# A hybrid decoder block on one core: GpSimd's elementwise work of the SSM stage moved to VectorE

## Chip, cores and metric

One core of one Trainium2 chip (trn2) runs the whole program in one launch. The metric is device time in microseconds (us), lower is better. Engines carry the names of the profile: PE (TensorE), PEld (its weight loads), DVE (VectorE), ACT (ScalarE), POOL (GpSimd) and SP (SyncE, which only issues DMAs here).

## What is computed

One decoder layer, 1024 tokens of 1024 features, all in float32. Cut to the parts that matter here:

```python
h = _rmsnorm(x, norm_mix_g[l])
z = h @ w_in[l]
q, k, v, f, u_ssm, g_attn, g_ssm = jnp.split(z, splits, axis=-1)
y_attn = _forgetting_attention(q, k, v, f + b_forget[l])
y_ssm = _s5(u_ssm, ...)
mixed = sigmoid(g_attn) * (y_attn @ w_proj_attn[l]) + sigmoid(g_ssm) * (y_ssm @ w_proj_ssm[l])
x = x + mixed @ w_out[l]
x = x + _hier_moe(...)
```

`_s5` is a diagonal state-space model of 32 groups, each with 16 channels and 64 complex states: x_t = A x_(t-1) + B u_t, y_t = Re(C x_t) + D u_t, then GELU and a gated linear unit. The two gates g_attn and g_ssm are 2 x 1024 columns of the first product.

## The kernel before

The program goes through stages: norm and the product for u and the forget gate; **the SSM stage**, in which the gate products also run; attention with its projections; the output projection and the router; the 32 experts. The change lies in the SSM stage, about 65 to 320 us of the trace.

Matrix products that must be exact use split operands. Each weight tile is cast on ACT to a high part (`wgh`, L149), and the remainder (`wgl`, raw minus high, L150) is a low part; a product is then three matmuls per block of 128 rows: high by high (L160), low by high (L161), high by low (L162), each 512 columns wide. `gate_run(m)` does this for 128 of the 2048 gate columns: 2 x 24 matmuls. The weights come in groups of 256 columns, as two raw tiles `raw_g` of 128 x 1024 values; `gate_split` casts and subtracts both, one subtraction on DVE and one on POOL. A group is split a group ahead, and its raw slots are then free for the next load, which SP issues (L103). The finished gate tile is copied out of PSUM on ACT (`ge`, L164) and stored by a DMA from ACT's queue (L165).

The state-space part runs in four blocks of 8 groups (here called the first to the fourth). Tiles of a block have one buffer each, so blocks follow each other. In a block:

- DVE makes phases `v` and `CO` (L518 to L525), with two wraps to a whole turn (L283, L284); ACT takes their sines (`SI` L524, `CO` L526). `w` shares its memory with `zc`, so the first wrap of a block waits until PE has read the `zc` of the block before.
- `outer` (L533 to L539) makes `HQ` (128 x 1152) and `PT` (128 x 1024): a product on DVE, a second product into `tq` on POOL (L538), and the sum on DVE.
- PE multiplies `HQ` (L551) into `Ka`, copied out by ACT (L554), corrected by DVE (L556) and spread into `Mt` by eight DMAs from POOL's queue (L558). PE transposes `PT` (L577), ACT copies it out as `Pm` (L581), and PE multiplies `Pm` with the inputs (L584).
- `turn` (L561 to L567) rotates this by the phases into `zin`, for each half of the block: products on DVE (L564, L566, the latter into `zt`) and the sum on POOL (L567). DVE scans `zin` along time (L596), `turn` rotates back into `zc`, and PE multiplies `Mt` and `zc` into the outputs (L604, L605), through GELU on ACT (L608).

A tile scheduler sets the order on every engine when the program is built, from its own estimate of times. On PE it puts the gate matmuls between those of the blocks. Each engine then runs its list strictly in that order: a matmul whose operand is late holds the gate matmuls behind it too.

Of the kernel before, what the change touches and what calls it, by code (L numbers as in the profile page):

```python
# [16 lines left out]
ALU = mybir.AluOpType  # L17
# [25 lines left out]
def hybrid_block(ctx: ExitStack, tc: tile.TileContext, t, out):  # L43

    nc = tc.nc
# [20 lines left out]
    def f32(ap):  # L66
        return ap.bitcast(F32)
# [4 lines left out]
    def slot(name, shape=(S,), dt=F32, where=None):  # L72
        pl, n = where or (slab, SLOTS)
        return pl.tile([P] + list(shape), dt, tag="s4", name=name, bufs=n)
# [69 lines left out]
    def gate_split(raws):  # L144
        ws = []
        for kh, raw in enumerate(raws):
            wh = slot("wgh", (4, 256), F32R)
            wl = slot("wgl", (4, 256), F32R)
            nc.scalar.copy(wh, raw)  # L149
            (nc.gpsimd if kh else nc.vector).tensor_tensor(wl, raw, f32(wh), ALU.subtract)  # L150
            ws.append((wh, wl))
        return ws

# [282 lines left out]
    def gate_run(m):  # L436

        g = m // 2
        if m % 2 == 0:
            if g + 1 not in gates and g + 1 < 8:  # L440
                gates[g + 1] = gate_split(raw_gs[g + 1])
            if g + 2 < 8:
                raw_gs.append(gate_load(g + 2))
        for n in range(2):
            gate_products(m, gates[g], n)
# [4 lines left out]
    for g in range(2):  # L450
        gates[g] = gate_split(raw_gs[g])
# [36 lines left out]
    with ExitStack() as st:  # L488
# [19 lines left out]
        for b in range(G // GB):  # L508
# [22 lines left out]
            tq = wp2.tile([P, GB, 9, CG], F32, name="tq", tag="t3")  # L531

            def outer(dst, ua, ca, ub, cb, op, n, n0):  # L533
                sh = [P, GB, n, CG]
                ub4 = lambda u_: u_[:, gs, n0:n0 + n].unsqueeze(3).to_broadcast(sh)
                cb4 = lambda c_: c_[:, gs, :].unsqueeze(2).to_broadcast(sh)
                nc.vector.tensor_tensor(dst, ub4(ua), cb4(ca), ALU.mult)
                nc.gpsimd.tensor_tensor(tq[:, :, 0:n, :], ub4(ub), cb4(cb), ALU.mult)  # L538
                nc.vector.tensor_tensor(dst, dst, tq[:, :, 0:n, :], op)  # L539

            outer(HQ, U1g, Cre, U2g, Cim, ALU.add, 9, 0)
            outer(PT, U1r, Bbr, U2r, Bbi, ALU.add, 8, 0)

            Mt = wp2.tile([P, GB, P], F32, name="Mt")
# [16 lines left out]
            def turn(dst, src, sl, op):  # L561
                zt = wp2.tile([P, 4, P], F32, name="zt", bufs=2)
                n = src.shape[2]
                nc.vector.tensor_tensor(dst, src, CO[:, sl, 0:n], ALU.mult)  # L564
                for o in (0, 64):
                    nc.vector.tensor_tensor(zt[o:o + 64, :, 0:n], src[64 - o:128 - o], SI[o:o + 64, sl, 0:n], ALU.mult)  # L566
                nc.gpsimd.tensor_tensor(dst, dst, zt[:, :, 0:n], op)  # L567


            zin = wp2.tile([P, GB, P], F32, name="zin")  # L570
# [1 line left out]
            for q4 in range(GB // 4):  # L572
                sl = slice(q4 * 4, q4 * 4 + 4)
                psp = smtile()
                for r in range(4):
                    g = q4 * 4 + r
                    nc.tensor.transpose(psp[:, r * P:(r + 1) * P],  # L577
                                        PT[:, g].rearrange("p t c -> p (t c)"), ident)
                v4 = lambda ap: ap.rearrange("p (a b) -> p a b", a=4)
                Pm = wp2.tile([P, 4, P], F32, name="Pm")  # L580
                nc.scalar.copy(Pm, v4(psp))  # L581
                px = smtile()
                for r in range(4):
                    nc.tensor.matmul(px[:, r * P:(r + 1) * P], Pm[:, r, :], uT[:, q4 * 4 + r, :],  # L584
                                     start=True, stop=True)
                turn(zin[:, sl, :], v4(px), sl, ALU.subtract)
# [6 lines left out]
            for q4 in range(GB // 4):  # L593
                sl = slice(q4 * 4, q4 * 4 + 4)
                rs = smtile()
                nc.vector.tensor_tensor_scan(rs, rho[:, sl].rearrange("p g j -> p (g j)"),  # L596
                                             zin[:, sl].rearrange("p g j -> p (g j)"),
                                             0.0, op0=ALU.mult, op1=ALU.add)
                turn(zc[:, sl, 1:P], v4(rs)[:, :, 0:P - 1], sl, ALU.add)
                ps = smtile()  # L600
                for r in range(4):
                    g = q4 * 4 + r
                    o = ps[:, r * P:(r + 1) * P]
                    nc.tensor.matmul(o, uT[:, g, :], Mt[:, g, :], start=True, stop=False)  # L604
                    nc.tensor.matmul(o, zc[:, g, :], HQ[:, g, 1:9, :].rearrange("p n c -> p (n c)"),  # L605
                                     start=False, stop=True)
                c0 = (g0 + q4 * 4) * CG
                nc.scalar.activation(  # L608
                    Yg[:, :, c0:c0 + 64].rearrange("p t (g c) -> p g t c", c=CG),
                    ps.rearrange("p (g t c) -> p g t c", g=4, t=8), AF.Gelu_apprx_tanh)  # L610
# [6 lines left out]
    with ExitStack() as st:  # L617
# [3 lines left out]
        for k in (0, 2):  # L621
            raw = slot("raw_l", (2, 512))
# [18 lines left out]
        for m in range(4):  # L641
            ms = slice(m * P, m * P + P)
            for n in range(2):
                ns = slice(n * 512, n * 512 + 512)
                ps = smtile()
                for k in range(4):
                    wh, wl = [w_[:, k % 2, ms] for w_ in wgl_[k // 2]]
# [870 lines left out]
```

## Time and profile before

| | |
|---|---|
| Three runs | 1191.03, 1191.19, 1195.45 us; median 1191.19 us |
| Profiled execution | 1195.19 us, its span 1193.5 us |
| Busy over the span | PE 1111.4 us (93%), DVE 795.3 (67%), ACT 620.3 (52%), POOL 431.3 (36%) |
| Granted PE clock, mean | 0.974 of full speed |

The profiled execution stands at the slow end of the three runs, 4.0 us above their median; the other 1.7 us beside the span are start and end of the launch. In the timeline a row is one instruction (or several alike, xN): start, duration, engine, line, operation, output and inputs, shapes; in brackets the time its engine stood idle before it and what ended that. A 512-column matmul shows 0.39 us but a new one starts every 0.23 us, as they are pipelined. The granted clock is a share of full speed: 1.00 is the 2.4 GHz level, 0.50 the 1.2 GHz level.

### The profile page before, as it was taken

The numbers are of one execution on the slowest core, as the hardware profiler recorded it, in microseconds if no ns is written. First come the engines' busy times: TensorE is split into PE (matmuls) and PEld (weight loads), VectorE is DVE, ScalarE is ACT, GpSimd is POOL, SyncE is SP. The second block draws the span as 40 slices with busy tenths as digits, with TensorE's granted clock in tenths as the row PEclk, the third lists the DMA queues.
The fourth block names the chain that finished last, engine by engine and source line by source line (L and its number), as shares of the span: only waits on it lengthen the run. The fifth ranks groups of instructions, "written<-read, shape, count | busy, mean of one in ns | idle before, by whom it ended". The sixth has DMA issues, their size and how long they took to land. (4 is left out here: it accounts for less than half of the span.)

```text
span 1193.5 us, 15934 instructions
## 1 busy us (share of the span) xinstructions
PE 1111.4 (93%) x5323; PEld 851.5 (71%) x5324; DVE 795.3 (67%) x1561; ACT 620.3 (52%) x1195; POOL 431.3 (36%) x431
## 2 busy tenths in 40 slices
PE   5999989899999999999899989998599999999995
PEld 4778877787898878888667767886366666666562
DVE  4976786575027889898986795538566666666661
ACT  5443232233226566756769453103466666666672
POOL 3143553541523564756624362103322222222211
PEclk9999999899999999999999998999699999999998
DMA  7625652330443020001523548564699999999992
GB/s 236 85 55 159 137 81 62 72 90 18 116 96 54 10 43 23 22 13 45 204 71 116 176 152 310 190 221 179 189 329 343 330 309 317 318 309 322 315 331 47
DMA packets 100918, 193.78 MB, mean 162 GB/s; under 512 B 26176, under 2 KB 55168, under 8 KB 100832
## 3 DMA queue, kind: packets, MB, share of 16 engines
q1 hardware_dynamic: 82176, 150.16, 41.1%
q0 software_dynamic: 14048, 34.17, 10.5%
q10 hardware_dynamic: 4608, 8.39, 1.9%
q8 instruction: 43, 0.70, 0.2%
q14 instruction: 43, 0.35, 0.1%
HBM read 164.30 MB, written 35.52 MB: 167 GB/s over the span
## 5 line engine op out<-in xcount | busy, mean ns | idle before, releaser
L1104 DVE TENSOR_TENSOR wel<-raw_e,weh 128x512 fp32r<-128x512 f32 x256 | 157.4, 687 | 118.1 <-ACT weh L1103 118.1
L1103 ACT CAST weh<-raw_e 128x512 fp32r<-128x512 f32 x256 | 137.1, 623 | 1.7 <-DMA raw_e<-in_w_expert_gate 1.3
L912 POOL TENSOR_TENSOR sm<-sm,pe 128x256 f32<-128x256 f32 (+2 forms) x80 | 96.3, 1204 | 69.5 <-ACT pe L909 61.3
L1379 PE MATMUL psA_t<-wd,hT 128*96 128x512 f32 x256 | 117.0, 600 | 2.7 <-DMA wd<-in_w_expert_down 1.9
L1354 PE MATMUL psA_t<-weh,xh 128*96 128x512 f32 x256 | 102.9, 402 | 0.2
L161 PE MATMUL psA_t<-hTh,wgl 128*128 128x512 f32 x256 | 101.8, 398 | 0.0
L160 PE MATMUL psA_t<-hTh,wgh 128*128 128x512 f32 x256 | 101.6, 397 | 0.0
L1355 PE MATMUL psA_t<-wel,xh 128*96 128x512 f32 x256 | 101.5, 396 | 0.0
L162 PE MATMUL psA_t<-hTl,wgh 128*128 128x512 f32 x256 | 101.3, 396 | 0.0
L1356 PE MATMUL psA_t<-weh,xl 128*96 128x512 f32 x256 | 100.6, 393 | 0.0
L1381 POOL DMA_INDIRECT out_rows<-R,ix x32 | 46.0, 1438 | 128.1 <-ACT hT L1370 116.9
L795 PE MATMUL psA_t<-wqh,hTh 128*128 128x384 f32 x256 | 87.9, 343 | 0.0
L796 PE MATMUL psA_t<-wql,hTh 128*128 128x384 f32 x256 | 86.3, 337 | 0.0
L797 PE MATMUL psA_t<-wqh,hTl 128*128 128x384 f32 x256 | 86.2, 337 | 0.0
L1330 POOL DMA_INDIRECT XG<-xn_d,ix x32 | 36.1, 1128 | 136.5 <-PE psB_t L1341 130.6
L1380 ACT ACTIVATE R<-psA_t,wts 96x512 f32<-96x512 f32 x64 | 43.8, 684 | 76.7 <-PE psA_t L1379 74.6
L1379 PEld LDWEIGHTS psA_t<-wd,hT 128*96 128x96 f32 x256 | 40.5, 168 | 55.6 <-issue 49.4
L907 ACT ACTIVATE pH<-psB_t 128x512 fp32r<-128x512 f32 (+1 forms) x96 | 49.2, 512 | 36.4 <-PE psB_t L904 36.2
L910 DVE TENSOR_TENSOR pL<-pe,pH 128x256 fp32r<-128x256 f32 (+2 forms) x80 | 63.0, 800 | 6.6 <-ACT pe L909 5.7
L160 PEld LDWEIGHTS psA_t<-hTh,wgh 128*128 128x128 f32 x256 | 48.5, 190 | 10.0 <-DVE uS L219 0.5
L161 PEld LDWEIGHTS psA_t<-hTh,wgl 128*128 128x128 f32 x256 | 48.7, 190 | 9.7 <-POOL wgl L150 0.2
L1163 PE MATMUL psA_t<-woh,mxh 128*128 128x512 f32 x128 | 54.3, 424 | 1.2 <-DVE gt L988 1.2
(427 smaller groups left out, 2867.8 us busy)
## 6 DMA issues: line engine op xcount, KB each, us to landing
raw_e<-in_w_expert_gate SPq DMA_DIRECT2D x64, 512.0 KB
raw_e<-in_w_expert_up SPq DMA_DIRECT2D x64, 512.0 KB
wd<-in_w_expert_down SPq DMA_DIRECT2D x64, 512.0 KB
gate_d<-ge ACTq DMA_DIRECT2D x32, 256.0 KB
gt<-gate_d SPq DMA_DIRECT2D x16, 512.0 KB
raw_g<-in_w_in SPq DMA_DIRECT2D x12, 512.0 KB
raw_q<-in_w_in SPq DMA_DIRECT2D x48, 128.0 KB
x<-in_x SPq DMA_DIRECT2D x8, 512.0 KB
```

The source lines that it names most:

```text
L160: nc.tensor.matmul(ps, wh, hTh[k][:, ns], start=(k == 0), stop=False)
L161: nc.tensor.matmul(ps, wl, hTh[k][:, ns], start=False, stop=False)
L162: nc.tensor.matmul(ps, wh, hTl[k][:, ns], start=False, stop=(k == KD - 1))
L795: nc.tensor.matmul(ps[:, :384], ah, wh, start=(k == 0), stop=False)
L796: nc.tensor.matmul(ps[:, :384], ah, wl, start=False, stop=False)
L912: nc.gpsimd.tensor_tensor(sm[:, o0:], sm[:, o0:], pe[:, :n], ALU.add)
L1103: nc.scalar.copy(wh[d_], src)
L1104: nc.vector.tensor_tensor(wl[d_], src, f32(wh[d_]), ALU.subtract)
L1354: nc.tensor.matmul(ps, xh[:, k, :], wh[:, k % 2, :], start=(k == 0), stop=False)
L1355: nc.tensor.matmul(ps, xh[:, k, :], wl[:, k % 2, :], start=False, stop=False)
L1356: last = nc.tensor.matmul(ps, xl[:, k, :], wh[:, k % 2, :], start=False, stop=(k == KD - 1))
L1379: pe = nc.tensor.matmul(po, hT[:, j, :], wd[j][:, ns], start=(j == 0), stop=(j == 1))
```

## The change

Three elementwise operations change engine; nothing else in the source does. The second `wgl` of each gate group, the second product of `outer` and the sum of `turn` go from POOL to DVE:

```diff
             nc.scalar.copy(wh, raw)
-            (nc.gpsimd if kh else nc.vector).tensor_tensor(wl, raw, f32(wh), ALU.subtract)
+            nc.vector.tensor_tensor(wl, raw, f32(wh), ALU.subtract)
...
                 nc.vector.tensor_tensor(dst, ub4(ua), cb4(ca), ALU.mult)
-                nc.gpsimd.tensor_tensor(tq[:, :, 0:n, :], ub4(ub), cb4(cb), ALU.mult)
+                nc.vector.tensor_tensor(tq[:, :, 0:n, :], ub4(ub), cb4(cb), ALU.mult)
                 nc.vector.tensor_tensor(dst, dst, tq[:, :, 0:n, :], op)
...
-                nc.gpsimd.tensor_tensor(dst, dst, zt[:, :, 0:n], op)
+                nc.vector.tensor_tensor(dst, dst, zt[:, :, 0:n], op)
```

POOL keeps the memsets of `Mt` and `zc`, the DMAs that fill `Mt`, and `yo` (L654). Because the scheduler orders anew, PE, DVE, ACT and POOL have other lists in this stage; SP's list is the same, and the stages after it are too.

DVE, third block, from the end of `HQ` to the end of `CO`. Before:

```order
L150 TENSOR_TENSOR wgl<-raw_g,wgh 128x1024
L520 TENSOR_TENSOR w<-phl,j_623 128x1024
L539 TENSOR_TENSOR PT<-PT,tq 128x1024
L521 TENSOR_TENSOR v<-w,v 128x1024
L522 TENSOR_SCALAR CO<-v 128x1024
L283 TENSOR_SCALAR w<-v 128x1024
L284 SCALAR_TENSOR_TENSOR v<-w,v 128x1024
L283 TENSOR_SCALAR w<-CO 128x1024
L284 SCALAR_TENSOR_TENSOR CO<-w,CO 128x1024
```

And with the change:

```order
L150 TENSOR_TENSOR wgl<-raw_g,wgh 128x1024
L520 TENSOR_TENSOR w<-phl,j_623 128x1024
L150 TENSOR_TENSOR wgl<-raw_g,wgh 128x1024
L521 TENSOR_TENSOR v<-w,v 128x1024
L538 TENSOR_TENSOR tq<-U2r,Bbi 128x8x128
L522 TENSOR_SCALAR CO<-v 128x1024
L283 TENSOR_SCALAR w<-v 128x1024
L539 TENSOR_TENSOR PT<-PT,tq 128x1024
L284 SCALAR_TENSOR_TENSOR v<-w,v 128x1024
L538 TENSOR_TENSOR tq<-U2g,Cim 128x1152
L283 TENSOR_SCALAR w<-CO 128x1024
L284 SCALAR_TENSOR_TENSOR CO<-w,CO 128x1024
```

Three instructions came in ahead of the last `CO`: the second `wgl`, the `tq` for `PT`, and the `tq` for the `HQ` of the fourth block.

PE, third block, from the products for `Ka` to the first that needs `Pm`. Before:

```order
L551 MATMUL psB_t<-HQ,Bst 16x128 x8
L577 MATMUL psB_t<-ident,PT 128x128 x4
L160 MATMUL psA_t<-hTh_134,wgh 128x512
L161 MATMUL psA_t<-hTh_134,wgl 128x512
L162 MATMUL psA_t<-hTl_142,wgh 128x512
L160 MATMUL psA_t<-hTh_135,wgh 128x512
L584 MATMUL psB_t<-uT,Pm 128x128 x4
```

And with the change:

```order
L551 MATMUL psB_t<-HQ,Bst 16x128 x8
L577 MATMUL psB_t<-ident,PT 128x128 x4
L160 MATMUL psA_t<-hTh_134,wgh 128x512
L161 MATMUL psA_t<-hTh_134,wgl 128x512
L162 MATMUL psA_t<-hTl_142,wgh 128x512
L160 MATMUL psA_t<-hTh_135,wgh 128x512
L161 MATMUL psA_t<-hTh_135,wgl 128x512
L162 MATMUL psA_t<-hTl_143,wgh 128x512
L160 MATMUL psA_t<-hTh_136,wgh 128x512
L161 MATMUL psA_t<-hTh_136,wgl 128x512
L584 MATMUL psB_t<-uT,Pm 128x128 x4
```

The first L584 stands four gate matmuls further back.

ACT, second block, from the sines to the two `Pm`. Before:

```order
L524 ACTIVATE SI<-v,sgn 128x1024
L164 COPY ge<-psA_t 128x512
L526 ACTIVATE CO<-CO 128x1024
L165 DMA gate_d<-ge 128x512
L149 CAST wgh<-raw_g 128x1024
L164 COPY ge<-psA_t 128x512
L149 CAST wgh<-raw_g 128x1024
L165 DMA gate_d<-ge 128x512
L554 COPY Ka<-psB_t 16x512 x2
L581 COPY Pm<-psB_t 128x512 x2
```

And with the change:

```order
L524 ACTIVATE SI<-v,sgn 128x1024
L526 ACTIVATE CO<-CO 128x1024
L164 COPY ge<-psA_t 128x512
L149 CAST wgh<-raw_g 128x1024
L165 DMA gate_d<-ge 128x512
L554 COPY Ka<-psB_t 16x512 x2
L581 COPY Pm<-psB_t 128x512
L149 CAST wgh<-raw_g 128x1024
L581 COPY Pm<-psB_t 128x512
```

One `wgh` cast went from ahead of the first `Pm` to behind it, and one `ge` to ahead of the sines. In the third block ACT's list has `ge` behind `CO` before, and ahead of `CO` with the change.

## Rows read from the trace of the kernel before

**Rows 1.** Windows view, one stretch: length; busy by engine; clock; DMA share; GB/s
```profile
core 0: us, PE busy (x) PEld busy (x) DVE busy (x) ACT busy (x) POOL busy (x), PEclk, DMA share, GB/s
200.00:220.00 20.00, 15.48 (x76) 12.84 (x75) 12.99 (x16) 4.80 (x7) 9.31 (x12) 0.83 0.28 65
```

**Rows 2.** PE's waits, 50 to 340 us: total, times, longest
```profile
PE psB_t L584 <- ACT Pm L581: 6.0, 2, 4.5
PE psB_t L604 <- DMA Mt<-Ka: 2.3, 1, 2.3
PE psB_t L605 <- POOL zc L567: 1.5, 2, 1.0
```

**Rows 3.** Timeline of PE, second and third block
```profile
161.88 1.16 PE L584 MATMUL psB_t<-uT,Pm 128*128 128x128 f32 x8 [1.48 <-ACT Pm L581]
...
165.12 0.48 PE L160 MATMUL psA_t<-hTh,wgh 128*128 128x512 f32 x1
...
179.01 0.77 PE L604 MATMUL psB_t<-Mt,uT 128*128 128x128 f32 x2 [2.30 <-DMA Mt<-Ka]
...
210.95 2.08 PE L584 MATMUL psB_t<-uT,Pm 128*128 128x128 f32 x8 [4.52 <-ACT Pm L581]
...
216.72 0.48 PE L162 MATMUL psA_t<-hTl,wgh 128*128 128x512 f32 x1
```

**Rows 4.** Instructions of single lines: duration in ns min/median/max, first and last start
```profile
L537 DVE TENSOR_TENSOR HQ<-U1g,Cre x4: 1337/1340/1359, 93.8 to 237.8; 128x1152 f32<-128x1152 f32 x4
L567 POOL TENSOR_TENSOR zc<-zc,zt x8: 1277/2256/2311, 128.6 to 270.4; 128x508 f32<-128x508 f32 x8
```

**Rows 5.** Timeline of DVE, 60 to 330 us
```profile
61.16 0.68 DVE L407 TENSOR_TENSOR bt<-Bre,sc 128x512 f32<-128x512 f32 x1
...
110.64 1.23 DVE L284 SCALAR_TENSOR_TENSOR CO<-w,CO 128x1024 f32<-128x1024 f32 x1
...
140.32 1.23 DVE L283 TENSOR_SCALAR w<-v 128x1024 f32<-128x1024 f32 x1 [3.13 <-PE psB_t L605]
...
148.17 1.23 DVE L539 TENSOR_TENSOR PT<-PT,tq 128x1024 f32<-128x1024 f32 x1 [1.82 <-POOL tq L538]
...
150.56 2.53 DVE L522 TENSOR_SCALAR CO<-v 128x1024 f32<-128x1024 f32 x1
...
155.72 1.23 DVE L284 SCALAR_TENSOR_TENSOR CO<-w,CO 128x1024 f32<-128x1024 f32 x1
...
187.02 1.23 DVE L283 TENSOR_SCALAR w<-v 128x1024 f32<-128x1024 f32 x1 [9.03 <-PE psB_t L605]
...
192.97 2.95 DVE L520 TENSOR_TENSOR w<-phl,j 128x1024 f32<-128x1024 f32 x1
195.85 3.41 DVE L539 TENSOR_TENSOR PT<-PT,tq 128x1024 f32<-128x1024 f32 x1
...
200.43 2.53 DVE L522 TENSOR_SCALAR CO<-v 128x1024 f32<-128x1024 f32 x1
...
205.59 1.23 DVE L284 SCALAR_TENSOR_TENSOR CO<-w,CO 128x1024 f32<-128x1024 f32 x1
...
224.26 1.23 DVE L150 TENSOR_TENSOR wgl<-raw_g,wgh 128x1024 fp32r<-128x1024 f32 x1 [5.02 <-ACT wgh L149]
...
246.88 0.69 DVE L522 TENSOR_SCALAR CO<-v 128x1024 f32<-128x1024 f32 x1
```

**Rows 6.** Timeline of ACT, first and third block
```profile
115.90 0.57 ACT L554 COPY Ka<-psB_t 16x512 f32<-16x512 f32 x1 [0.45 <-PE psB_t L551]
...
206.85 1.06 ACT L526 ACTIVATE CO<-CO 128x1024 f32<-128x1024 f32 x1 [0.83 <-DVE CO L284]
...
210.33 0.57 ACT L581 COPY Pm<-psB_t 128x512 f32<-128x512 f32 x1
```

**Rows 7.** First of eight DMAs into Mt, second and third block: KB, us to landing
```profile
Mt<-Ka POOLq DMA_DIRECT2D x1, 64.0 KB, 12.6
...
Mt<-Ka POOLq DMA_DIRECT2D x1, 64.0 KB, 2.2
```

**Rows 8.** The page's part 2, DMA engines: busy tenths in 40 slices
```profile
DMA  7625652330443020001523548564699999999992
```

## The prediction

> **What bounds the kernel now.** I read the profile from the coarse view to the fine one. The busy shares say that PE works 93% of the span; but a share is a mean over stages, so I went to the stage that the change touches. In the windows view the reader should see that even at its worst PE is the fullest engine there: in the 20 us from 200 it is busy 15.48 us, DVE 12.99, POOL 9.31 [rows 1]. In most of the other 20 us stretches from 80 to 280 us PE has no idle time at all. So in this stage time is lost only where PE stands still, or runs at a lower clock; what DVE and POOL take costs nothing until PE waits for it.
>
> The list of PE's waits names three such places in the four blocks [rows 2]: for `Pm` twice, 6.0 us together; once for the DMAs into `Mt`, 2.3 us; twice for `zc`, 1.5 us. PE's timeline shows where they fall: 1.48 us in the second block and 4.52 us in the third for `Pm`, 2.30 us in the second for `Mt` [rows 3]. The long ones cost more than their idle time. After the 4.52 us, PE did the same work from L584 on (sixteen L584 matmuls, four transposes, four gate matmuls) in 216.72 - 210.95 = 5.77 us that took 165.12 - 161.88 = 3.24 us in the second block, and the granted clock, 0.83 of full speed in the mean of the window, was at the lower of its two levels (1.2 GHz) for a part of it [rows 1, 3]. That is 2.5 us more, behind a time in which PE did nothing. After the 1.48 us wait nothing of the kind shows.
>
> Why is `Pm` late? `Pm` is a copy on ACT, and ACT's list has the sine of `CO` ahead of it, which waits for DVE's last `CO`: in the third block DVE ends it at 205.59 + 1.23 = 206.8, ACT starts at 206.85, and `Pm` is reached at 210.33 [rows 5, 6]. So the chain is DVE, then ACT, then PE. DVE needs 19.8 us for it, from the first wrap at 187.02 (the moment PE lets go of `zc`) to 206.8 [rows 5].
>
> **What the change does to this chain.** DVE gets more work. By its own rows a product of 128 x 1152 takes 1.34 us there [rows 4], one of 128 x 1024 1.23 us (the sum of `PT` at 148.17) and one of 128 x 512 0.68 us [rows 5]; one behind another starts some 0.1 us sooner than these durations say. All four blocks together receive 4 x (1.34 + 1.23) for `tq`, 16 x 0.68 for the sums of `turn` and 8 x 1.23 for `wgl`: 31 us over the stage, where DVE stands idle 7 of the 20 us of [rows 1] alone. Capacity is not the question, only what lies in the chain.
>
> *Third block.* Into the stretch of 19.8 us come one `wgl` and two `tq`, about 1.1 + 1.1 + 1.3 = 3.5 us. But three of its instructions took far longer than their kind: 2.95, 3.41 and 2.53 us where others of the same shape took 1.21, 1.23 and 0.69 [rows 5]. They are the three beside which POOL ran `tq` or `wgl`; L522 took 2.53 us in the second and third blocks with a `tq` beside it, and 0.69 us in the fourth, where POOL had none [rows 5]. With POOL's arithmetic gone I take the excess of 5.8 us as gone. The bounds are 0 and 5.8; I choose the upper, as the fourth block is the changed case in all but name. So 19.8 - 5.8 + 3.5 = 17.5, and `CO` is 2.3 us earlier. On ACT, 210.33 - 206.85 = 3.5 us pass from `CO` to `Pm` [rows 6]; the sine takes 1.06 of them and two copies of `Ka` about 1.1, and the remaining 1.4 us belong to `ge` and its store. `ge` is now ahead of `CO`, where its product is done, so I take the 1.4 us off. `Pm` is then 3.7 us earlier. PE wants it four gate matmuls later, 4 x 0.23 = 0.9 us. Together 4.6 us against a wait of 4.52 us: the wait goes, and with it the 2.5 us at the lower clock. As the two sides are that near, I leave 0.4 us as a remainder.
>
> *Second block.* From 140.32 to 155.72 + 1.23 = 16.6 us. Two `tq` add 2.4; the wait for POOL's `tq` (1.8) and the excess of L522 (1.8) go [rows 5]: 15.4 us, 1.2 us earlier. One `wgh` cast stands behind `Pm` now, 1 us more. The wait of 1.48 us goes.
>
> *First and fourth block.* In the first, `CO` comes some 1.3 us later by the same kind of sum, but DVE ended it at 111.9 and ACT's copies of `Ka`, ahead of `Pm`, waited for PE until 115.90 [rows 5, 6]: hidden by PE's gate matmuls, with 115.9 - 111.9 - 1.06 for the sine = 2.9 us to spare. If PE came sooner there, `Pm` would be late in this block too. The fourth has no `tq` for a next block, and `Pm` is not waited for.
>
> *The sums of turn.* POOL took 2256 ns for one [rows 4], DVE 0.68 us. The four sums per block add 2.7 us to DVE, but the chain from L584 to `zc` gets shorter: POOL's sums stood behind its DMA issues and a `wgl`. PE's new list asks for the first `zc` about six matmuls earlier than before, 1.4 us. In the third block I get the second `zc` 0.4 us late, in place of 1.5 us of waits [rows 2]; in the other blocks it comes in time.
>
> *The low parts of the gate weights* are a group ahead of their products, so PE does not wait for them; two of them before the first block lie in time that DVE spends waiting for ACT. Cost nothing, as long as DVE keeps that cover.
>
> *Mt.* Its DMAs stay in POOL's queue. In the second block the first landed after 12.6 us, in the third after 2.2 us [rows 7]; in the second, two loads of `raw_g` ran beside it. Those loads start when `wgl` frees a slot, so they move with the chain, and I keep the wait of 2.3 us as it is. The bounds are gone (a gain of 2.3, and up to 2.5 for the clock, as at the other long wait) and 2.7 us longer. A rule speaks against the change here: the Trainium skill (SBUF — State Buffer, section SBUF: two separate sides) says that the descriptors of a DMA from POOL's queue are written by GpSimd, which VectorE locks out while it runs certain two-port instructions. [...]
>
> **Sum.** 1.5 + 4.5 + 2.5 + 1.5 - 0.4 - 0.4 = 9.2 us. Against the profiled execution: 1195.2 - 9.2 = 1186.0 us. That execution is 4.0 us over the median of the runs; which stall it has that the others lack can't be seen, and it may be `Mt`, which I count as unchanged. Against the median: 1191.2 - 9.2 = **1182.0 us**. After the stage every list is the same, so I expect the rest only to start earlier.
>
> **Rivals.**
> 1. *Mt is late in more blocks.* Both `wgl` of a group now run close together, so two loads of `raw_g` start together, and may meet the `Mt` copies in the first and third block as they did in the second. For it: 12.6 against 2.2 us [rows 7]. Against it: in the first block the same meeting cost no wait. Two more waits of 2.3 us with up to 2.5 us of slow clock are 4.6 to 9.6 us: 1186.6 to 1191.6, centre 1189.
> 2. *A cast holds DVE (slower).* `wgl` waits for ACT's `wgh`. DVE stood 5.02 us for one at 224.26 [rows 5]; the second of the pair waited on POOL, where little was behind it. Now both stand in DVE's list between the parts of `turn`, so that a late cast delays `zc`, and PE. It decides if casts come over 1 us later than DVE reaches them. At 5.0 us idle and 2.5 us of slow clock, in the first and third block, this costs 15 us: 1191.2 - 9.2 + 15 = 1197. Against it: with PE's long wait gone, the slot for the cast is free about 7 us sooner, before DVE arrives.
> 3. *The gain is swallowed later.* The DMA engines are busy 90% or more in nine of the last ten slices [rows 8]; if the expert loads do not start sooner, the end stays: 1191. Against it: they wait for slots that earlier work frees, and that moves along.
>
> **How the numbers follow.** Forecast 0.66, rival 1 0.16, rival 2 0.10, rival 3 0.08. The forecast's own range is 1177 (the `Mt` wait gone too, 4.8 us) to 1186 (half of the third block's `Pm` wait and slow clock left, 3.5 us); to leave out no more than 2 in 10, the range has to reach over rival 1: 1176 to 1190. A measurement of this kernel tells about 0.5%, 6.0 us, from no change. The forecast is faster by more than that (0.66); rivals 1 and 3 lie within (0.24); rival 2 is slower (0.10).
>
> **What would show it.** Right: PE's waits for `Pm` and for `zc` are each under 1 us, no stretch of low clock around the third block's L584, L522 at 0.69 us in all blocks, the span of the third block's chain on DVE near 17.5 us. Wrong: L522 still at 2.5 us (then the long rows were not POOL's doing, and `CO` is 3.5 us later); waits of DVE for `wgh` inside `turn`; new waits of PE for `Mt`; or a stage that ends 9 us earlier and a total that does not.

## The result and the profile after

The changed kernel takes **1180.22 us** in the median (6 runs, 1177.96 to 1186.2), the kernel before 1193.43 us (6 runs, 1191.03 to 1195.45): a ratio of 0.9891, with a 95% interval of 0.9867 to 0.9915, so it is 0.9 to 1.3% faster. The forecast was 1182.0 us, faster. The profiled execution took 1180.84 us, against 1195.19 before.

Where the time came from is read from the start of three groups of PE: the first product for `Ka` (L551, first block), the first projection of attention (L795) and the first product of the experts (L1354). After, by single lines (duration in ns, count, first and last start, form):

```profile
L551 PE MATMUL psB_t<-HQ,Bst x64: 272/273/284, 113.7 to 240.6; 128*16 128x128 f32 x64
L795 PE MATMUL psA_t<-wqh,hTh x256: 331/335/423, 319.3 to 558.7; 128*128 128x384 f32 x128
L1354 PE MATMUL psA_t<-weh,xh x256: 387/397/740, 838.0 to 1156.8; 128*96 128x512 f32 x128
```

And before:

```profile
L551 PE MATMUL psB_t<-HQ,Bst x64: 272/273/283, 114.8 to 255.2; 128*16 128x128 f32 x64
L795 PE MATMUL psA_t<-wqh,hTh x256: 331/334/423, 334.2 to 574.2; 128*128 128x384 f32 x128
L1354 PE MATMUL psA_t<-weh,xh x256: 387/394/742, 852.9 to 1171.0; 128*96 128x512 f32 x128
```

From L551 to L795, the SSM stage (called its length below), it is 319.3 - 113.7 = 205.6 us in place of 219.4: 13.8 us less. The experts start 14.9 us sooner, the span ends 14.3 us sooner. So nearly all of the gain in these two executions arises in the stage that was changed, and all but 0.6 us of it is carried to the end.

PE's waits after, 50 to 340 us (the answer to [rows 2]): those for `Pm` and `zc` are gone, that for `Mt` is half of what it was.

```profile
PE psB_t L604 <- DMA Mt<-Ka: 1.2, 1, 1.2
```

The windows after, with the columns of [rows 1]: in the stretch from 200 us PE is busy all 20 us in place of 15.48, POOL 4.58 in place of 9.31, and the granted clock is 1.00 in place of 0.83.

```profile
160.00:180.00 20.00, 18.82 (x101) 15.73 (x99) 15.27 (x22) 4.04 (x6) 2.88 (x6) 1.00 0.67 91
200.00:220.00 20.00, 20.00 (x108) 17.08 (x107) 16.67 (x23) 6.82 (x10) 4.58 (x8) 1.00 0.44 86
```

The chain on DVE in the third block, after (the answer to [rows 5]):

```profile
181.46 1.24 DVE L283 TENSOR_SCALAR w<-v 128x1024 f32<-128x1024 f32 x1 [5.70 <-PE psB_t L605]
...
187.42 1.21 DVE L520 TENSOR_TENSOR w<-phl,j 128x1024 f32<-128x1024 f32 x1
188.56 1.21 DVE L150 TENSOR_TENSOR wgl<-raw_g,wgh 128x1024 fp32r<-128x1024 f32 x1
...
190.82 1.21 DVE L538 TENSOR_TENSOR tq<-U2r,Bbi 128x1024 f32<-128x1024 f32 x1
191.96 0.68 DVE L522 TENSOR_SCALAR CO<-v 128x1024 f32<-128x1024 f32 x1
...
193.16 1.21 DVE L539 TENSOR_TENSOR PT<-PT,tq 128x1024 f32<-128x1024 f32 x1
...
195.43 1.35 DVE L538 TENSOR_TENSOR tq<-U2g,Cim 128x1152 f32<-128x1152 f32 x1
...
197.42 1.22 DVE L284 SCALAR_TENSOR_TENSOR CO<-w,CO 128x1024 f32<-128x1024 f32 x1
```

The three long rows are now 1.21 (L520), 1.21 (L539) and 0.68 us (L522); before they were 2.95, 3.41 and 2.53. From the first wrap to the end of `CO` it is 198.64 - 181.46 = 17.2 us in place of 19.8, with three instructions more in it. ACT starts `CO`'s sine at 198.68 and, with `ge` now ahead of it, reaches `Pm` 1.9 us later in place of 3.5 [rows 6]:

```profile
198.68 1.06 ACT L526 ACTIVATE CO<-CO 128x1024 f32<-128x1024 f32 x1 [0.55 <-DVE CO L284]
...
200.60 0.57 ACT L581 COPY Pm<-psB_t 128x512 f32<-128x512 f32 x1
```

`Pm` is done at 200.60 + 0.57 = 201.17, and PE takes it without a wait, 0.46 us later, when its list comes to it:

```profile
201.63 1.05 PE L584 MATMUL psB_t<-uT,Pm 128*128 128x128 f32 x8
```

So not all of the third block's gain is DVE's. The chain gave 19.8 - 17.2 = 2.6 us, ACT's list with `ge` ahead of `CO` gave 3.5 - 1.9 = 1.6, and the four gate matmuls that PE's list now has ahead of L584 gave 0.9: about half of it comes from the new order.

### The profile page after: what moved, and what is told of

It is laid out like the page before. It is cut to its first block, busy times and chain, and to the rows that moved or that the text cites. A ratio compares the mean times of both kernels' runs of the same rounds, so it can differ in the third digit from the quotient of the medians.

```text
span 1179.2 us, 15928 instructions
## 1 busy us (share of the span) xinstructions
PE 1106.0 (94%) x5323; PEld 848.4 (72%) x5324; DVE 804.9 (68%) x1593; ACT 620.3 (53%) x1195; POOL 356.9 (30%) x399
## 3 DMA queue, kind: packets, MB, share of 16 engines
q0 software_dynamic: 14048, 34.17, 10.6%
## 5 line engine op out<-in xcount | busy, mean ns | idle before, releaser
L1354 PE MATMUL psA_t<-weh,xh 128*96 128x512 f32 x256 | 103.8, 406 | 0.2
L795 PE MATMUL psA_t<-wqh,hTh 128*128 128x384 f32 x256 | 88.0, 344 | 0.0
L164 ACT COPY ge<-psA_t 128x512 f32<-128x512 f32 x32 | 18.7, 584 | 86.6 <-PE psA_t L162 81.8
L857 DVE TENSOR_REDUCE mx<-psB_t 128x1 f32<-128x512 f32 (+2 forms) x96 | 51.2, 551 | 6.2 <-PE psB_t L855 2.7
```

The costliest lines, as they stand in the source:

```text
L795: nc.tensor.matmul(ps[:, :384], ah, wh, start=(k == 0), stop=False)
L1354: nc.tensor.matmul(ps, xh[:, k, :], wh[:, k % 2, :], start=(k == 0), stop=False)
```

## Experiments

Theory A: POOL's arithmetic stretches the DVE instructions beside it, DVE's chain to `CO` ends late, and through ACT's list `Pm` and PE are late. The main rival, B: the new lists alone do it, as the change moved PE's and ACT's instructions too. Ratios stand against runs of the kernel before on the same chip; "length" is that of the stage as above, from one profiled execution each (two of the changed kernel gave 205.6 and 205.8).

| kernel | median us | ratio, 95% interval | length us |
|---|---|---|---|
| tq alone | 1182.79 | 0.9922, 0.9889 to 0.9955 | 206.9 |
| turn sums alone | 1192.16 | 0.9994, 0.9972 to 1.0016 | 215.3 |
| second wgl alone | 1193.3 | 0.9995, 0.9974 to 1.0016 | 217.5 |
| tq and turn sums | 1180.41 | 0.9891, 0.9866 to 0.9916 | 206.2 |
| changed, 12 idle POOL products a block | 1200.21 | 1.005, 1.0022 to 1.0078 | 225.3 |
| the same, in 24 pieces | 1192.1 | 0.9982, 0.9959 to 1.0006 | 215.4 |
| before, CO's sine behind Pm | 1191.53 | 0.9982, 0.9957 to 1.0007 | 213.7 |
| changed, once more | 1183.75 | 0.9912, 0.9894 to 0.993 | 205.8 |
| changed, Mt copies by SP | 1179.87 | 0.9877, 0.9859 to 0.9895 | 208.1 |
| the same, yo on DVE too | 1181.46 | 0.9911, 0.9877 to 0.9946 | 208.1 |
| changed, q3 on DVE too | 1214.49 | 1.0182, 1.0149 to 1.0214 | 205.7 |
| changed, yo, q3, gt on DVE too | 1214.22 | 1.0157, 1.0135 to 1.0178 | 206.0 |

### One line of the change at a time

**tq alone.**

```diff
-                nc.gpsimd.tensor_tensor(tq[:, :, 0:n, :], ub4(ub), cb4(cb), ALU.mult)
+                nc.vector.tensor_tensor(tq[:, :, 0:n, :], ub4(ub), cb4(cb), ALU.mult)
```

> Only the second product of outer (tq, L538) goes to DVE; the turn sums and the second wgl stay on POOL. Theory A (POOL's arithmetic beside DVE stretches DVE's chain to the last CO, and Pm is late by that): the long L522 of 2.53 us falls to 0.69 in the second and third blocks and the wait for tq goes; a wgl of POOL still stands beside DVE in the third block, so one row there stays long. Chain on DVE: second block about 15.4 us (16.6 before), third about 18 to 18.5 (19.8 before). PE's waits for Pm: second block gone, third under 1.5 us, little of the lower clock; the waits for zc (1.5 us) and Mt (about 2) stay. 5 to 8 us below before: 1185 to 1188. Theory B (the new lists of PE do it, with more gate matmuls ahead of the first L584, whatever DVE does): the same for Pm, as 7 gate matmuls now stand ahead of it in the third block, but the chain keeps its 16.6 and 19.8 us.

Measured: 10.6 us below before by the medians, more than the 5 to 8 expected. By the ratios (0.78 of 1.09%) and by the medians (10.6 of 13.2 us) that is some three quarters of the whole change. The chain came out at 198.47 - 180.10 = 18.4 us in the third block and 15.0 in the second, as expected by A; B would have kept 19.8 and 16.6. The third block's wait for `Pm` fell by 3.1 us, and the chain is 1.4 of these; the rest came with the new order, three gate matmuls more ahead of L584 and a shorter stretch of ACT from `CO` to `Pm` (2.4 us in place of 3.5). PE waits, 50 to 340 us:

```profile
PE psB_t L584 <- ACT Pm L581: 1.4, 1, 1.4
...
PE psB_t L605 <- POOL zc L567: 0.6, 2, 0.5
```

There was no wait for `Mt` here, which A had not expected. One long row is left, and with POOL's row beside it one can see how it becomes long. DVE:

```profile
186.06 1.21 DVE L520 TENSOR_TENSOR w<-phl,j 128x1024 f32<-128x1024 f32 x1
187.19 3.41 DVE L538 TENSOR_TENSOR tq<-U2r,Bbi 128x1024 f32<-128x1024 f32 x1
```

And POOL:

```profile
186.23 3.29 POOL L150 TENSOR_TENSOR wgl<-raw_g,wgh 128x1024 fp32r<-128x1024 f32 x1 [5.44 <-ACT wgh L149]
```

POOL's `wgl` starts while L520 runs, and L520 ends at 187.27. `wgl` ends at 189.52, 2.25 us behind that, and DVE's `tq` at 190.60, 1.1 us behind `wgl`. Each of the three lasts about its own time after the one ahead of it has ended: they ran one behind another.

In the first block of the same run it was POOL that waited. Its row, and the last of the DVE instructions beside it:

```profile
106.05 7.50 POOL L150 TENSOR_TENSOR wgl<-raw_g,wgh 128x1024 fp32r<-128x1024 f32 x1 [18.86 <-ACT wgh L149]
```

```profile
110.07 1.22 DVE L518 TENSOR_TENSOR v<-phh,j 128x1024 f32<-128x1024 f32 x1
```

`wgl` started while L539 ran on DVE; four more DVE instructions then ran at their usual lengths, the last of them ended at 111.29, and `wgl` ended at 113.55, 2.26 us behind it. What decides which engine goes first, no run here shows.

**The sums of turn alone.**

```diff
-                nc.gpsimd.tensor_tensor(dst, dst, zt[:, :, 0:n], op)
+                nc.vector.tensor_tensor(dst, dst, zt[:, :, 0:n], op)
```

> Only the sums of turn (L567) go to DVE. The lists around Pm are those of before. Theory A: the waits for zc on POOL (1.5 us, and some 0.6 us of slow clock behind them) go, those for Pm (6.0 us and 2.5 us of slow clock) stay, as tq and wgl are still POOL's: 1190 to 1192, within 0.3% of before. Theory C (POOL's queue is the matter: with the 2.26 us sums gone from it, tq and the Mt DMAs start sooner): Pm's waits shrink to under 3 us and the Mt wait goes too, 1184 to 1187.

Measured: no difference that the runs can tell, as A said; C is out. The waits for `zc` went, those for `Pm` stayed to the tenth:

```profile
PE psB_t L584 <- ACT Pm L581: 6.0, 2, 4.5
PE psB_t L604 <- DMA Mt<-Ka: 2.0, 1, 2.0
```

The 0.6 us of slow clock that A put behind the waits for `zc` was not there: from 220 to 240 us, where they lie, the granted clock of before was 1.00.

The profiled execution was the fastest of its 12 (1186.45 us), so the length of 215.3 flatters this kernel. Behind its wait for `Mt` the granted clock stays at 1.00 in both windows from 160 to 200 us, where the profiled execution of before had this:

```profile
160.00:180.00 20.00, 16.22 (x79) 13.13 (x78) 15.51 (x19) 4.87 (x8) 13.75 (x13) 0.97 0.80 107
180.00:200.00 20.00, 20.00 (x100) 17.04 (x99) 12.98 (x8) 6.25 (x8) 7.72 (x4) 0.94 0.24 56
```

So in that execution of before the wait for `Mt` had a stretch at the lower clock behind it, which here, with nearly the same wait, did not come.

**The second wgl alone.**

```diff
-            (nc.gpsimd if kh else nc.vector).tensor_tensor(wl, raw, f32(wh), ALU.subtract)
+            nc.vector.tensor_tensor(wl, raw, f32(wh), ALU.subtract)
```

> Only the second wgl of each gate group goes to DVE. The lists of PE around Pm are those of before. Theory A: of the three long rows in the third block the two that a wgl on POOL stretched (L520 2.95 us, L539 3.41 us) fall to about 1.23 us, at 1.1 us for the wgl now on DVE: chain 19.8 - 3.9 + 1.1 = 17.0 us if POOL's tq stays as it is, and the third block's wait for Pm falls from 4.5 to about 2 us, the second block's 1.5 us stays: 3 to 5 us below before, 1188 to 1190. Theory B (lists): no change, 1193, with the Pm wait of 4.5 us still there. Theory D (the casts: wgl on DVE holds DVE for wgh): DVE waits of several us for wgh and a time over before.

Measured: no change, a miss for A, which had asked for 1188 to 1190; the time is the one that B had named, though the third block's wait for `Pm`, which B kept at 4.5 us, is 3.5. DVE, third block:

```profile
191.38 2.95 DVE L520 TENSOR_TENSOR w<-phl,j 128x1024 f32<-128x1024 f32 x1
...
197.66 0.68 DVE L522 TENSOR_SCALAR CO<-v 128x1024 f32<-128x1024 f32 x1
198.26 2.64 DVE L283 TENSOR_SCALAR w<-v 128x1024 f32<-128x1024 f32 x1
```

The row of 3.41 us became 1.21, but L520 kept its 2.95 us, and POOL's second `tq`, which had held L522, now held the wrap behind it (2.64 in place of 0.68). The chain is 204.15 - 185.42 = 18.7 us in place of 17.0. I had put two long rows down to `wgl`; only one was its doing. The `Pm` wait of the third block fell by 1.0 us, about what the chain had lost (1.1), and here the lists of PE and ACT around it are those of before. But the waits for `zc` grew from 1.5 to 2.8:

```profile
PE psB_t L584 <- ACT Pm L581: 5.0, 2, 3.5
PE psB_t L605 <- POOL zc L567: 2.8, 2, 1.7
```

Theory D falls by the time, which did not go over before, but not wholly by its mechanism: ahead of the scans of the third block DVE's list now has two `wgl` that wait for casts (4.98 and 1.12 us, at 220.55 and 222.90), where before it had one (5.02), and in the stage DVE waits 10.1 us for `wgh` in place of 8.8.

**tq and the turn sums, without the wgl.**

> tq (L538) and the sums of turn (L567) on DVE, the second wgl left on POOL: the change without its first line. Theory A: tq alone gave 10.6 us by the medians, the turn sums some 1 us, the wgl on DVE the rest: 1180 to 1183, with Pm's wait of 1.4 us (third block, DVE held for a wgl of POOL there) as in the run with tq alone and no wait for zc. Theory D (a wgl on DVE costs, as DVE then waits for casts): 1 to 3 us below the changed kernel.

Measured: 1180.41, the same as the whole change in the two measurements of it (1180.22, 1183.75). The wait of 1.4 us for `Pm` is there as in the run with `tq` alone, and none for `zc` is listed. The first line of the change neither gives nor costs anything that these runs can tell.

### The lists of the changed kernel with work on POOL

To part A from B, POOL gets arithmetic again while every list of PE, ACT and DVE in the stage stays that of the changed kernel (the edit is written out over several lines, and what places the products right behind the memset is left out):

```diff
             nc.gpsimd.memset(Mt, 0.0)
+            sh = [P, 2, 9, CG]
+            for z in range(12):
+                nc.gpsimd.tensor_tensor(idle, U2g[:, pair(z), :].unsqueeze(3).to_broadcast(sh),
+                                        Cim[:, pair(z), :].unsqueeze(2).to_broadcast(sh), ALU.mult)
```

> The changed kernel, with twelve products of 128 x 288 on POOL in each block, behind the memset of Mt, into a tile that nobody reads: added work beside DVE's chain with no wait put on anybody, and the lists of PE, ACT and DVE in this stage those of the changed kernel. Theory A: every DVE instruction beside them stretches as L522 (0.69 to 2.53), L520 (1.23 to 2.95) and L539 (to 3.41) did before; some 9 us of POOL work per block lengthen the chain (17.2 us in the third block) by 4 to 9 us, PE waits for Pm again in three blocks, 4 us or more each, with the lower clock behind it: 8 to 20 us over the changed kernel, 1188 to 1200. Theory B (the lists do it) and any account by waits alone: the DVE rows keep 0.69 and 1.23 us, no wait for Pm, 1180 within 3 us; the Mt DMAs, behind these products in POOL's queue, are not needed before the products have ended.

Measured: 1200.21 us, slower than before, with lists under which the changed kernel is faster than before. So the lists alone do not do it; that they have a share, the rows of the third block show above, and no run has the new lists with just the POOL work of before. PE waits 12.6 us for `Pm` in three blocks (4.6, 4.7, 3.2), and the granted clock is 0.83 in two windows, from 160 and from 200 us, and 0.86 in the one from 260:

```profile
PE psB_t L584 <- ACT Pm L581: 12.6, 3, 4.7
```

The twelve products of the second block on POOL, and DVE beside them:

```profile
139.75 18.24 POOL L545 TENSOR_TENSOR idle<-U2g,Cim 128x288 f32<-128x288 f32 x12
```

```profile
150.23 1.70 DVE L539 TENSOR_TENSOR PT<-PT,tq 128x1024 f32<-128x1024 f32 x1
151.85 1.17 DVE L522 TENSOR_SCALAR CO<-v 128x1024 f32<-128x1024 f32 x1
```

The rows are longer by the same 0.48 us, whether they are long (1.22 to 1.70) or short (0.69 to 1.17). The chain of the third block is 210.65 - 187.67 = 23.0 us: 5.8 more than without, or twelve times 0.48.

**The same number of elements in 24 pieces** (against the run with twelve, written out in the same way).

```diff
-            sh = [P, 2, 9, CG]
-            for z in range(12):
+            sh = [P, 1, 9, CG]
+            for z in range(24):
```

> As the run with twelve idle products of 128 x 288 on POOL in each block of the changed kernel, but cut into 24 of 128 x 144, the same number of elements. Theory A1 (POOL and DVE take turns, one instruction of each): every DVE row beside them is longer by one POOL piece, so by about 0.24 us in place of 0.48 (L522 at 0.93, two-input rows at 1.46), the third block's chain is some 20 to 20.7 us (23.0 with pieces of 0.48, 17.2 without), PE's waits for Pm fall below the 12.6 us there, and the time is 5 to 15 us under that run's 1200. Theory A2 (the two share a bandwidth, and each slows in proportion to what the other moves): the same stretch as before the cut, 0.48 us for a long row, a chain of 23 us, 1200.

Measured, third block, POOL and DVE:

```profile
186.25 25.18 POOL L545 TENSOR_TENSOR idle<-U2g,Cim 128x144 f32<-128x144 f32 x24
```

```profile
197.99 0.92 DVE L522 TENSOR_SCALAR CO<-v 128x1024 f32<-128x1024 f32 x1
...
199.67 1.45 DVE L539 TENSOR_TENSOR PT<-PT,tq 128x1024 f32<-128x1024 f32 x1
```

A DVE row is now longer by 0.23 us, the chain is 206.21 - 185.58 = 20.6 us, and the time is 8 us under the run with twelve pieces: A1 in all three numbers, A2 in none. In these two runs the engines take turns, and a DVE instruction pays a fixed price for one POOL instruction, however long it is itself. The price is not all of POOL's row. The shortest of the products, in the run with twelve and in the run with 24 pieces (duration in ns, shortest, median and longest), took 0.68 and 0.43 us, and DVE's rows grew by 0.20 us less:

```profile
L545 POOL TENSOR_TENSOR idle<-U2g,Cim x48: 677/1538/1810, 85.8 to 253.6; 128x288 f32<-128x288 f32 x48
```

```profile
L545 POOL TENSOR_TENSOR idle<-U2g,Cim x96: 428/1291/1654, 84.8 to 253.9; 128x144 f32<-128x144 f32 x96
```

The Trainium skill (SBUF — State Buffer, section SBUF: two separate sides) calls the port pair that the two share an exclusive lock that is held for a whole instruction, not a split of bandwidth. These two runs agree that it is no split: each row grew by 0.48 or by 0.23 us, whatever its own length.

### The link through ACT

`Pm` does not need `CO`; it stands behind it in ACT's list. In the kernel before, with nothing moved from POOL (the edit written out over several lines):

```diff
-            nc.scalar.activation(CO, CO, AF.Sin, scale=-TWO_PI)
...
-                nc.scalar.copy(Pm, v4(psp))
+                pm = nc.scalar.copy(Pm, v4(psp))
+                if q4 == 0:
+                    with tc.issue_after(pm.ins):
+                        nc.scalar.activation(CO, CO, AF.Sin, scale=-TWO_PI)
```

> The kernel before, all work on its old engines and DVE's list unchanged; only ACT's sine of CO (L526) is put behind the first copy Pm of each block, so that Pm no longer stands behind DVE's chain. Theory A (PE loses its time because Pm, which does not need CO, waits in ACT's list behind CO): the waits of PE for Pm (6.0 us) and the lower clock behind them (2.5 us) go though POOL's arithmetic still stretches DVE's rows (2.95, 3.41, 2.53 us stay); the waits for Mt and zc stay, or grow by a microsecond: 1185 to 1188. Theory H (Pm is only the first of several things that come late when DVE is slow: the turn needs CO right behind it): the loss moves to the waits for zc, and the time stays at 1191 or over.

Measured: the time is H's (1191 or over), the waits are neither theory's. `zc` was waited for no more than before, against H. But `Pm` was still waited for, in more places and nearly as long (5.2 us in place of 6.0), against A:

```profile
PE psB_t L584 <- ACT Pm L581: 5.2, 3, 2.4
PE psB_t L605 <- POOL zc L567: 1.5, 2, 1.0
```

ACT's timeline of the third block, where 2.2 us of the 4.5 were left, shows why: the sine of `SI`, which needs the last but two of DVE's rows, is still ahead of `Ka` and `Pm`.

```profile
200.73 1.15 ACT L524 ACTIVATE SI<-v,sgn 128x1024 f32<-128x1024 f32 x1 [4.88 <-DVE v L284]
...
204.31 0.57 ACT L581 COPY Pm<-psB_t 128x512 f32<-128x512 f32 x1
```

The length did fall by 5.7 us (213.7), but most of that is another wait: the one for `Mt`, 2.3 us, is not there, nor the stretch at the lower clock behind it. PE's list and ACT's casts moved with the edit, so it is not the sine alone. In the median 2.4 us are left, with an interval that holds no change. The profiled execution lost again in the experts what the stage had gained: they start 6.6 us sooner than before, and the span is 0.8 us shorter. The third block's wait went from 4.5 to 2.2 us with ACT's new order, as it should if that order carries part of the loss; how much of the total it carries stays open.

### More work for DVE, and Mt by another queue

**The changed kernel once more**, as a measure for the runs that shared its chip.

> The changed kernel once more, so that the other three of this call stand beside it on one chip: 1180 within 3 us, PE's waits for Pm and zc under 1 us.

1183.75 us: 3.5 us over the first measurement and just outside the 3 us expected around 1180, with the same waits in the stage (`Mt` 1.3 us, none for `Pm` or `zc`).

**yo, q3 and gt on DVE too** (L654, L811, L989, each `nc.gpsimd` to `nc.vector`).

> The changed kernel with three more kinds of POOL arithmetic on DVE: yo (L654) at the end of the SSM stage, the scaling q3 (L811) in the projections of attention and the sum gt (L989) in front of the output projection. Theory A (POOL's arithmetic takes turns with DVE's, and DVE does the same work in less time): DVE's rows there get shorter too; where PE waits for DVE in those stages it gains, 0 to 6 us below the changed kernel: 1174 to 1180. Theory E (outside the SSM stage DVE is the fuller engine, and more work on it makes PE wait): 2 to 6 us over it.

**q3 alone** (L811).

> The changed kernel with only the scaling q3 (L811) of attention's projections moved to DVE. In attention DVE is busy 33 to 37 of 40 us in each stretch, against 15 to 34 in the SSM stage. Theory E (where DVE is that full, POOL's turn is cheaper than DVE's time, and PE waits for DVE): most of the wide version's 30 us is here, 1195 to 1212, with PE's waits for mx, QY and pe longer. Theory A alone (fewer turns for POOL is always better): 1180 or under; then the loss came from gt or yo.

Measured: 1214.22 and 1214.49 us; the one line of q3 makes the whole loss of 30 us, all of it behind the SSM stage, whose length is unchanged. Slower is what theory E had said, but the loss lies beyond both of its ranges (2 to 6 us; 1195 to 1212), and its reason does not hold: DVE is less busy than in the changed kernel (315.9 us from 320 to 720 us, against 322.2). The product itself is shorter on DVE. In the changed kernel, and then with q3 on DVE:

```profile
L811 POOL TENSOR_TENSOR qk<-qk,rstd x32: 603/613/943, 329.0 to 567.1; 128x256 f32<-128x256 f32 x32
```

```profile
L811 DVE TENSOR_TENSOR qk<-qk,rstd x32: 406/426/1529, 328.6 to 593.2; 128x256 f32<-128x256 f32 x32
```

But it needs `rstd`, which POOL makes (L809, 1.03 us) in a queue of its own. Behind it on POOL the product waited for nobody else; in DVE's list it stops all that stands behind it. DVE's waits with q3 on DVE, 360 to 600 us, a line that the changed kernel has not got:

```profile
DVE qk L811 <- POOL rstd L809: 17.0, 18, 2.2
```

And PE's, 320 to 720 us, where the first was 0.6 us and the second 4.4 in the changed kernel:

```profile
PE psB_t L862 <- DVE mx L857: 7.4, 4, 2.5
PE acc L887 <- DVE pL L910: 6.1, 8, 1.7
```

That the wait for `rstd` is the cause was read from the trace, not tried: the scheduler also ordered attention anew.

**The Mt copies issued by SP**, and the same with yo on DVE.

```diff
-                nc.gpsimd.dma_start(Mt[CG * tau:CG * tau + CG, :, CG * tau:],
+                nc.sync.dma_start(Mt[CG * tau:CG * tau + CG, :, CG * tau:],
```

> The changed kernel with the eight DMAs into Mt per block issued by SP in place of POOL. Theory F (what is left of the Mt wait, 1.2 us, and the 2.3 us of before come from POOL's queue): Mt lands within 3 us of its issue, no wait of PE for Mt, 1.2 us or more below the changed kernel: 1177 to 1179. Theory G (the late landing comes from loads of raw_g that run at the same time, whoever issues; and in SP's list the copies stand in line with those loads): landings up to 12 us stay, PE waits as long or longer, 1180 or over. The scheduler orders PE's and DVE's work anew behind the first block here, so only the landing times settle it, not the total alone.

> The changed kernel with the Mt DMAs on SP's queue and yo (L654) on DVE. In the stretch from 280 to 320 us DVE is busy 6.6 of 40 us and POOL 14.9, and yo takes POOL 1.3 us each. Theory A: like the kernel with the Mt DMAs on SP alone (1179.9) or 1 us better, as PE does not wait for yo: 1178 to 1181. Theory E (the 30 us that the wide version lost come from yo, whose place in DVE's list delays the start of attention): 1190 or over.

Measured: 1179.87 and 1181.46 us. PE no longer waits for `Mt`, which speaks for F, but the lists changed, and it waits for `zc` in four places instead:

```profile
PE psB_t L605 <- DVE zc L567: 1.8, 4, 0.7
```

The trace gives no landing times for SP's queue, so F and G can't be told apart by them. 1179.87 is the lowest median of all and 3.9 us under the changed kernel on the same chip; but the stage is 2.3 us longer (208.1), and the gain lies in the experts, whose code is the same. I do not call it a better kernel: its interval overlaps that of the changed one. yo on DVE changed nothing that shows.

## Why the prediction was right

**What bounds.** PE stood still in this stage at the places named, and when those waits went the time went: right. The waits for `Pm` and `zc` and the low clock of the third block were undone; that for `Mt` was halved.

**The chain of the third block.** 17.5 us were forecast, 17.2 came; 15.4 in the second block, 15.0 came. The choice of the upper bound (all 5.8 us of excess go) was right, and the runs with idle products show why: POOL's instruction beside DVE's makes the row long. The estimate for DVE's own rows held: 1.21 for `wgl`, 1.21 and 1.35 for `tq`, 0.68 to 0.69 for L522 in all blocks. The two other terms, ACT's 1.4 us and PE's 0.9, came as 1.6 and 0.9.

**The terms.** `Pm` 1.5 and 4.5 us, the low clock of 2.5 us and `zc` 1.5 us all came, without the two remainders of 0.4 us. The term that was mis-sized is `Mt`, "kept as it is": its wait fell from 2.3 to 1.2 us, and the low clock behind it in the profiled execution of before (0.03 and 0.06 of 20 us: some 1.8 us) is gone; the last figure is an estimate from the two windows. 1.5 + 4.5 + 2.5 + 1.5 + 1.1 + 1.8 = 12.9 us, of 13.8 in the stage; the rest stays open, and so does what made the wait for `Mt` shorter. So the sum of 9.2 us was about 4 us short of the 13.2 us between the medians. The forecast of 1182.0 lies nearer to 1180.22 than that because it started from a low base: the three runs of before had a median of 1191.19, all six 1193.43. From these, the same sum gives 1184.2: that the forecast came within 2 us is in part luck.

**Why that execution stood 4.0 us above the median.** Of three runs, that is; above the median of all six it stood 1.8 us. The prediction said that it may be `Mt`. The run with the turn sums alone has nearly the same wait without the low clock, so up to 1.8 us can be that; it is not shown.

**The rule on descriptors.** It does not speak against this change. What the Trainium skill says in the section that the prediction names (SBUF — State Buffer, section SBUF: two separate sides) is about two-port instructions; the section lists instructions with two inputs in SBUF, as DVE's sums `zc<-zc,zt` are, apart from these, and has them contend only with a GpSimd instruction that reads SBUF. The bound of 2.7 us longer for `Mt` is shown by no run either: the wait became shorter. The median landing of the copies did go from 2.3 to 3.1 us, but it went to 4.0 in the run with `CO`'s sine behind `Pm`, where DVE had got no work, and no run isolates it.

**The rivals.** 1 (Mt late in more blocks): one wait of 1.2 us, refuted. 2 (a cast holds DVE): DVE waited 5.3 us for `wgh` in five places, the longest of them, 2.09 us, between a scan and the `turn` behind it, close to what the prediction had named as a sign of being wrong. But PE never waited for `zc`: refuted here as a loss, but q3 later showed DVE held by another partner, in a kernel that lost 30 us. 3 (swallowed later): the experts start 14.9 us sooner and the span ends 14.3 us sooner.

**What was not seen.** That `tq` alone is some three quarters of it, and that the `wgl`, which the prediction charged and credited in the third block's chain, gives nothing by itself: POOL's next instruction then meets DVE's next, and the waits for `zc` grow.

## What to carry to other kernels

Where VectorE and GpSimd both have elementwise work, look at single rows: rows of one shape with two lengths (0.69 and 2.53 us here), the long ones beside GpSimd's rows, are a sign that one engine waits for the other. A GpSimd instruction can then cost VectorE more than doing that work itself: a `tq` on GpSimd made L522 1.84 us longer, and VectorE does that `tq` in 1.35. It only matters on a chain that the bound engine waits for, so find that chain first (VectorE, then ScalarE's list, then TensorE). Before an instruction is moved into a list that runs strictly in order, look at where its operands come from: one that waited harmlessly behind its producer on GpSimd stopped all of VectorE 18 times in 240 us of attention, in a kernel that lost 30 us.

## What was not expected of the hardware

Smaller pieces of the same POOL work cost DVE less: beside products of 0.68 us each DVE row grew by 0.48 us, beside products of half the elements by 0.23, and the third block's chain was 20.6 us in place of 23.0. But the turns are not strict: in the run with `tq` alone one `wgl` on POOL took 7.50 us while DVE ran on. A plain memset on POOL seems to hold DVE as well; no run takes it away, but the first wrap of the third block took 1.24 us beside this one (1.23 before), and that of the first block, with no memset beside it, 0.69:

```profile
181.20 0.95 POOL L545 MEMSET Mt<- 128x1024 f32 x1 [18.32 <-PE psB_t L604]
```

And the stage of the experts, whose lists are the same in before and after, took from its first product to the end of the span 340.6 us before, 341.2 after, and 345.7 in the changed kernel once more: differences of 4 us in the total can arise there, whatever was done in the SSM stage.
